# A two-layer streaming encoder on one core: pair matrices and S5 outputs come later, and the last branch's first half is merged between gate products

## The chip, the core and the metric

The kernel runs on one core of a Trainium2 chip, as one program. The engines are TensorE (PE in the profile, its weight loads PEld), VectorE (DVE), ScalarE (ACT), GpSimd (POOL) and SyncE (SP), which issues the loads of the weights. The metric is the device time of one execution in microseconds, and a kernel's time is the median of its runs.

## The reference, cut to what matters

Two layers work on x of 256 rows and 1024 columns. Each layer adds half a feed-forward block, a mixer of four branches, and half a feed-forward block again. The change is in the mixer:

```
def layer_mixer(x):                       # D = 1024, 256 rows, chunk 64
    h = rmsnorm(x, mix_norm[l])
    p = h @ w_in[l]                       # 8*256 columns for the branches + 4*1024 for the gates
    u_a, u_b, r_p, k_p, v_p, z_in, b_g, c_g, gate_pre = jnp.split(p, SPLIT_POINTS, axis=-1)
    y_a = s5_mixer(u_a, ...)              # complex linear recurrence along time, then outputs
    y_b = pool_mixer(u_b, ...)
    y_c = rwkv7_mixer(h, r_p, k_p, v_p, ...)   # delta rule; pairwise products inside a chunk
    y_d = short_conv_mixer(z_in, b_g, c_g, conv_w[l])   # b_g * conv3(c_g * z_in)
    branches = einsum('bsgc,gcd->bsgd', stack([y_a, y_b, y_c, y_d]), w_branch[l])
    gates = sigmoid(gate_pre.reshape(b, s, 4, D))
    merged = sum(branches * gates, axis=2)
    return x + merged @ w_out[l]
```

The branches are numbered 0 (S5), 1 (pool), 2 (RWKV) and 3 (convolution).

## The kernel before

All large products are in fp32, which the kernel makes from two parts: a rounded one (h) and the rest (l). One k-step of 128 rows is three matmuls of 512 columns (`mm3`, L256 to L258): wh with xh, wl with xh, wh with xl. A weight unit is two k-steps of one 512-column half of a weight matrix. SP loads it into one of five raw buffers; ScalarE rounds it to wh (`convert`, L250); `finish` subtracts to get wl, as a rule on VectorE (`tt`, L225). The 256 rows are two tiles t = 0 and 1, and each unit is used by both: four k-steps in all. Four PSUM banks named acc collect these products. Four more, called by `bank()` (pb, gm, sY, tmA and so on), are taken in turn by everything else, so that a new one waits for the reader of the one four before it. Every wl, mg, gate, Gm and Hs instruction that goes through `tt` shows as L225.

The order of the work is made by a planner, `Flow`. It walks a list of steps, one for each unit and row tile, and each k-step is a tick. Beside the steps run threads, generators that give up control and name when they want it back: `wA(n)` n steps later, `wM(n, banks)` n ticks later and only if so many banks are free. What a thread issues stands in every engine's queue at that place. The queues run in order, so an instruction that waits holds all that stand behind it on its engine.

The mixer's steps are the columns of w_in for the branches, two blocks of 256 at a time (the last is bg and cg, the convolution's two gates), then for b = 3, 1, 0, 2 `gate_steps(b)` (the gate's product, two halves hf of 512 columns, with a sigmoid on ScalarE) and `branch_steps(b)` (the projection of the branch by w_branch, two halves). `merge` multiplies a projection with its gate and adds it to mg; for the last branch it then transposes mg and splits it into xh and xl, from which `down` takes the product with w_out.

Threads named in what follows:

- RWKV: W and BK are made on VectorE; the pair matrices gm (L1066) come in two rounds of two banks, sixteen small matmuls each; VectorE masks them into Gm, and POOL copies diagonal blocks into dg (L1077), from which the inverse (inv, L1097) is made much later. tmA and tmB (L1118, L1119) are two rounds of eight transposes; the copies RH (VectorE) and UV (ScalarE) read tmA.
- S5: gA, gB and gt are products on VectorE, followed by two scans (L1373), two products on POOL (gA by TC, gB by TS), Hs on VectorE, and the outputs sY on PE (L1389) in two halves.
- Convolution: zc is cg times z_in on VectorE; cv (L1498) is the sum over three taps, then cv times bg; yl is the rest part of a branch's output.

Of the kernel before, what the change touches and what calls it, by code (L numbers as in the profile page):

```python
# [70 lines left out]
def wM(n=1, banks=0):  # L71

    return ("M", n, banks)
# [98 lines left out]
def trunk_kernel(ctx: ExitStack, tc: tile.TileContext, a, out, dbg=None):  # L172
# [184 lines left out]
    def down(W, nk, lh, ll, scale, gain):  # L357
        P = {}
        ss = {}

        def go(t, hf, u):
            def f():
                if (t, hf) not in P:
                    P[t, hf] = acc()
                    if t not in ss:
                        ss[t] = small.tile([128, 2], F32, name=f"ss{t}", tag=f"ss{t}")
                mmu(P[t, hf], lh(t), ll(t), u, nk)
                if u.k0 + u.nk == nk:
                    args = (t, hf, P[t, hf], scale, ss[t])
                    spawn(next_input(*args, gain) if gain else last_norm(*args))  # L370
            fl.step(f, [u])

        pooled = (1, 3, (0, 0), (2, 0)) if nk == 8 else ()

        def unit(i, k0, hf):
            return Unit(W, k0, 2, hf * 512, 512, gp if i in pooled else ve)

        for k0 in range(0, nk - 4, 2):
            for hf in range(2):
                u = unit((k0, hf), k0, hf)  # L380
                for t in range(2):
                    go(t, hf, u)
        ends = [(hf, unit(i, k0, hf)) for i, (hf, k0) in enumerate((hf, k0) for hf in range(2) for k0 in (nk - 4, nk - 2))]
        if gain:
            for hf, u in ends:
                for t in range(2):
                    go(t, hf, u)
        else:
            for t in range(2):
                for hf, u in ends:  # L390
                    go(t, hf, u)
# [399 lines left out]
    def mixer(l):  # L791
# [110 lines left out]
        def rwkv():  # L902
# [152 lines left out]
            dg = small_tile("dg")  # L1055
            maskb = cc("mask").unsqueeze(1).to_broadcast([128, 4, 128])
            for j in range(2):
                yield wM(4 if j == 0 else 4, 2)
                ps = [bank("gm").rearrange("p (c t) -> p c t", c=4) for _ in range(2)]
                for c in range(4):  # L1060
                    m, o = c // 2, c % 2
                    for e in range(2):
                        es = slice(64 * e, 64 * e + 64)
                        lhs = BK[es, 2 * j + m, 2 * o:2 * o + 2].rearrange("p k t -> p (k t)")
                        rhs = W[es, 2 * j + m, 0:3:2] if o == 0 else W[es, 2 * j + m, 4:6]
                        pe.matmul(ps[e][:, c], lhsT=lhs, rhs=rhs, start=True, stop=True)  # L1066
                yield wA(1)
                for e in range(2):
                    h = 2 * j + e
                    g_ = et([128, 4, 128], f"Gm{h}")  # L1070
                    tt(g_, ps[e], maskb)
                    free()
                    Gm.append(g_)
                    gv = g_.rearrange("p (m o) s -> p o m s", o=2)
                    for q in range(4):
                        qs, cs = slice(32 * q, 32 * q + 32), slice(32 * (q % 2), 32 * (q % 2) + 32)
                        gp.tensor_copy(dg[qs, 2 * h:2 * h + 2], gv[qs, q // 2, :, cs])  # L1077
# [245 lines left out]
        def s5():  # L1323
# [54 lines left out]
            tt(gB, gB, TS, eng=gp)  # L1378
            yield wA(3)
            tt(Hs[:, :, 1:32], gA[:, :, 0:31], gB[:, :, 0:31], ALU.subtract)  # L1380
            yield wM(4, 1)
            pY = bank("sY").rearrange("p (u c) -> p u c", u=4)
            for u in range(4):
                if u == 2:
# [123 lines left out]
        gts = {}  # L1508
        mg = {}

        def gate_steps(b):
            for hf in range(2):
                P = {}

                def ev(t, hf, P):
                    yield wA(1)
                    g_ = st["mp"].tile([128, 512], F32, name="gate", tag="gate", bufs=NG)
                    sc.activation(g_, P[t], AF.Sigmoid, scale=rstd[t])
                    gts[b, t, hf] = g_

                for k0 in range(0, 8, 2):
                    u = Unit(Win, k0, 2, 2048 + b * D + hf * 512, 512)
                    for t in range(2):
                        def f(t=t, u=u, hf=hf, P=P):
                            if t not in P:
                                P[t] = acc()
                            mmu(P[t], lxh(t), lxl(t), u, 8)
                            if u.k0 == 6:
                                spawn(ev(t, hf, P))
                        fl.step(f, [u])  # L1530

        def merge(b, t, hf, p, first, lastb):
# [13 lines left out]
            p = bank()  # L1546
            transposes(p, m_, 4)
            yield wA(1)
            split(xs(xh, t)[:, 4 * hf:4 * hf + 4], xs(xl, t)[:, 4 * hf:4 * hf + 4], p.rearrange("p (a q) -> p a q", q=128))
            free()  # L1550

        def branch_steps(b, first=False, lastb=False):
            for hf in range(2):
                u = Unit(a["w_branch"][l, b], 0, 2, hf * 512, 512)
                for t in range(2):
                    def f(t=t, hf=hf, u=u):
# [16 lines left out]
        branch_steps(1)  # L1573
        gate_steps(0)
        branch_steps(0)
        gate_steps(2)
        branch_steps(2, lastb=True)
        down(a["w_out"][l], 8, lxh, lxl, 1.0, ("ffn2_norm", l))
        fl.step(es_.close, work=False)


# [97 lines left out]
```

## Time and profile before

| | us |
|---|---|
| runs | 1270.63, 1266.59, 1267.92 |
| median | 1267.92 |
| profiled execution | 1268.96 |
| its span, first to last instruction | 1267.2 |

| engine | busy us | share of the span |
|---|---|---|
| PE | 1241.1 | 98% |
| PEld | 1011.4 | 80% |
| DVE | 759.2 | 60% |
| ACT | 618.7 | 49% |
| POOL | 385.1 | 30% |

Times in the rows are counted from the start of the span. Layer 0's mixer does what is changed from about 270 to 310 and from 415 to 440, layer 1's 623 us later. In a timeline row stand the start, the duration, the engine, the line, the operation, the tile written and the tiles read; a bracket at the end gives the idle time before it and what ended it. Matmul rows overlap, since the next one starts while the one before drains: from start to start they take less than the durations say.

### The profile page before, as it was taken

The numbers are of one execution on the slowest core, as the hardware profiler recorded it, in microseconds if no ns is written. First come the engines' busy times: TensorE is split into PE (matmuls) and PEld (weight loads), VectorE is DVE, ScalarE is ACT, GpSimd is POOL, SyncE is SP. The second block draws the span as 40 slices with busy tenths as digits, with TensorE's granted clock in tenths as the row PEclk, the third lists the DMA queues.
The fourth block names the chain that finished last, engine by engine and source line by source line (L and its number), as shares of the span: only waits on it lengthen the run. The fifth ranks groups of instructions, "written<-read, shape, count | busy, mean of one in ns | idle before, by whom it ended". The sixth has DMA issues, their size and how long they took to land.

```text
span 1267.2 us, 19245 instructions
## 1 busy us (share of the span) xinstructions
PE 1241.1 (98%) x7472; PEld 1011.4 (80%) x7472; DVE 759.2 (60%) x935; ACT 618.7 (49%) x787; POOL 385.1 (30%) x512
## 2 busy tenths in 40 slices
PE   7999999999999999999999999999899999999997
PEld 6888878877778788888888888888667787888886
DVE  6955656488556565555465565465974666555543
ACT  5454445655445455443454444466554454544433
POOL 4694383153132310000079453204501233000001
PEclk9999999989999999999999999999999999999999
DMA  8676656544436566666666666566344465666662
GB/s 263 167 223 176 188 161 177 181 128 123 129 117 199 168 182 185 191 175 195 185 186 193 173 186 187 157 189 177 100 126 127 148 184 164 205 190 175 182 198 67
DMA packets 139667, 216.29 MB, mean 171 GB/s; under 512 B 30092, under 2 KB 42232, under 8 KB 139576
## 3 DMA queue, kind: packets, MB, share of 16 engines
q1 hardware_dynamic: 138296, 213.63, 57.1%
q10 hardware_dynamic: 1120, 1.40, 0.3%
q8 instruction: 58, 0.95, 0.3%
q0 software_dynamic: 160, 0.05, 0.1%
q14 instruction: 33, 0.27, 0.1%
HBM read 212.29 MB, written 1.57 MB: 169 GB/s over the span
## 4 chain that ended last, share of the span: by engine, by line
PE 93%; DVE 4%; issue 1%; POOL 1%; DMA 1%; ACT 0%; POOLq 0%; SPq 0%; DVEq 0%; ACTq 0%
PE acc L256 29%; PE acc L258 28%; PE acc L257 28%; PE pb L268 3%; PE inv L1097 1%; DVE wl L225 1%; POOL dg L1077 1%; DVE cv L1498 1%; DVE W L225 0%; PE sY L1389 0%; PE pb L771 0%; DVE rk L1026 0%; DVE mg L225 0%; DMA vr<-in_ffn_norm_dram 0%; PE wu L1202 0%
## 5 line engine op out<-in xcount | busy, mean ns | idle before, releaser
L225 DVE TENSOR_TENSOR wl<-raw,wh 128x1024 fp32r<-128x1024 f32 (+1 forms) x390 | 498.0, 1278 | 302.1 <-ACT wh L250 294.4
L250 ACT ACTIVATE wh<-raw 128x1024 fp32r<-128x1024 f32 (+1 forms) x393 | 414.6, 1056 | 418.7 <-PE acc L258 406.2
L256 PE MATMUL acc<-wh,xh 128*128 128x512 f32 (+1 forms) x1248 | 491.7, 394 | 0.0
L257 PE MATMUL acc<-wl,xh 128*128 128x512 f32 (+1 forms) x1248 | 475.1, 381 | 0.6 <-DVE wl L225 0.6
L258 PE MATMUL acc<-wh,xl 128*128 128x512 f32 (+1 forms) x1248 | 475.1, 381 | 0.0
L256 PEld LDWEIGHTS acc<-wh,xh 128*128 128x128 f32 x1248 | 236.0, 189 | 46.6 <-issue 5.1
L258 PEld LDWEIGHTS acc<-wh,xl 128*128 128x128 f32 x1248 | 236.0, 189 | 45.7
L257 PEld LDWEIGHTS acc<-wl,xh 128*128 128x128 f32 x1248 | 236.5, 190 | 40.9 <-DVE wl L225 1.1
L258 PE MATMUL acc<-wh,hl 128*128 128x512 f32 x352 | 138.7, 394 | 0.0
L256 PE MATMUL acc<-wh,hh 128*128 128x512 f32 x352 | 138.2, 393 | 0.0
L257 PE MATMUL acc<-wl,hh 128*128 128x512 f32 x352 | 138.0, 392 | 0.0
L225 POOL TENSOR_TENSOR wl<-raw,wh 128x1024 fp32r<-128x1024 f32 x11 | 26.4, 2398 | 241.5 <-ACT wh L250 241.5
L256 PEld LDWEIGHTS acc<-wh,hh 128*128 128x128 f32 x352 | 66.1, 188 | 15.2 <-issue 1.3
L257 PEld LDWEIGHTS acc<-wl,hh 128*128 128x128 f32 x352 | 66.2, 188 | 14.6
L258 PEld LDWEIGHTS acc<-wh,hl 128*128 128x128 f32 x352 | 66.2, 188 | 13.3
L429 DVE SCALAR_TENSOR_TENSOR hd<-acc,rs,sg 128x512 f32<-128x512 f32 (+1 forms) x48 | 33.7, 703 | 38.3 <-PE acc L258 36.5
L333 POOL TENSOR_SCALAR pre<-ss 128x1 f32<-128x1 f32 x2 | 0.4, 223 | 173.7 <-ACT junk L281 173.7
L221 ACT ACTIVATE hh<-pb 128x512 fp32r<-128x512 f32 (+1 forms) x48 | 27.0, 563 | 45.4 <-PE pb L268 45.4
L222 DVE TENSOR_TENSOR hl<-pb,hh 128x512 fp32r<-128x512 f32 (+1 forms) x48 | 31.0, 646 | 27.9 <-ACT hh L221 27.5
L225 POOL TENSOR_TENSOR mg<-mg,gate 128x512 f32<-128x512 f32 x16 | 29.9, 1886 | 50.8 <-DVE gate L225 50.8
L422 ACT ACTIVATE sg<-acc,rs 128x512 f32<-128x512 f32 (+1 forms) x48 | 31.1, 653 | 17.8 <-PE acc L258 16.8
L314 ACT ACTIVATE xh<-xg 128x512 fp32r<-128x512 f32 x24 | 15.2, 632 | 30.6 <-DVE xg L225 30.4
(341 smaller groups left out, 1105.5 us busy)
## 6 DMA issues: line engine op xcount, KB each, us to landing
raw<-in_w_in_dram SPq DMA_DIRECT2D x96, 512.0 KB
raw<-in_ffn_w_up_dram SPq DMA_DIRECT2D x88, 512.0 KB
raw<-in_ffn_w_down_dram SPq DMA_DIRECT2D x88, 512.0 KB
raw<-in_ffn_w_gate_dram SPq DMA_DIRECT2D x87, 512.0 KB
raw<-in_w_branch_dram SPq DMA_DIRECT2D x16, 512.0 KB
raw<-in_w_out_dram SPq DMA_DIRECT2D x16, 512.0 KB
x<-in_x_dram SPq DMA_DIRECT2D x2, 512.0 KB
raw<-in_rwkv_g_dram SPq DMA_DIRECT2D x8, 128.0 KB
```

The costliest lines, as they stand in the source:

```text
L221: sc.activation(dh, src, AF.Copy)
L222: eng.tensor_tensor(out=dl, in0=src, in1=dh.bitcast(F32), op=ALU.subtract)
L225: eng.tensor_tensor(out=o, in0=i0, in1=i1, op=op)
L250: sc.activation(self.h, self.r, AF.Copy)
L256: pe.matmul(ps, lhsT=lh, rhs=wh, start=first, stop=False)
L257: pe.matmul(ps, lhsT=lh, rhs=wl, start=False, stop=False)
L258: pe.matmul(ps, lhsT=ll, rhs=wh, start=False, stop=last)
L268: pe.transpose(b[:, j * 128:(j + 1) * 128], src[:, j * 128:(j + 1) * 128], ident)
L314: sc.activation(dh, xg, AF.Copy)
L422: sc.activation(sg[:, :n], pg[:, :n], AF.Silu, scale=rstd[t])
L429: ve.scalar_tensor_tensor(out=hd[:, :n], in0=pu[:, :n], scalar=rstd[t], in1=sg[:, :n], op0=ALU.mult, op1=ALU.mult)
L1077: gp.tensor_copy(dg[qs, 2 * h:2 * h + 2], gv[qs, q // 2, :, cs])
```

## The change

It has four parts.

1. `down`: the list `pooled` is gone. For w_out (`nk == 8`) four units per layer had their wl made on POOL; now all are made on VectorE.
2. Pair matrices: the first round of gm waits for ten ticks and not four, `wM(10, 2)`.
3. S5 outputs: sY waits for nine ticks and not four, `wM(9, 1)`.
4. `gate_steps` and `branch_steps` take the halves to do. Gate 2's first half is done alone; inside gate 2's second half, ahead of its third unit, the first half of branch 2 is projected and merged; its second half follows. The first half's merged result is split into two new tiles `mo` and not into xh and xl, which gate 2's second half still reads; `down` reads `mo` for k below 4.

```diff
-        pooled = (1, 3, (0, 0), (2, 0)) if nk == 8 else ()
 
         def unit(i, k0, hf):
-            return Unit(W, k0, 2, hf * 512, 512, gp if i in pooled else ve)
+            return Unit(W, k0, 2, hf * 512, 512)
...
             for j in range(2):
-                yield wM(4 if j == 0 else 4, 2)
+                yield wM(10 if j == 0 else 4, 2)
                 ps = [bank("gm").rearrange("p (c t) -> p c t", c=4) for _ in range(2)]
...
             tt(Hs[:, :, 1:32], gA[:, :, 0:31], gB[:, :, 0:31], ALU.subtract)
-            yield wM(4, 1)
+            yield wM(9, 1)
             pY = bank("sY").rearrange("p (u c) -> p u c", u=4)
...
-        def gate_steps(b):
-            for hf in range(2):
+        def gate_steps(b, halves=(0, 1), between=None):
+            for hf in halves:
                 P = {}
...
                 for k0 in range(0, 8, 2):
+                    if between and k0 == 4:
+                        between()
                     u = Unit(Win, k0, 2, 2048 + b * D + hf * 512, 512)
...
             p = bank()
             transposes(p, m_, 4)
             yield wA(1)
-            split(xs(xh, t)[:, 4 * hf:4 * hf + 4], xs(xl, t)[:, 4 * hf:4 * hf + 4], p.rearrange("p (a q) -> p a q", q=128))
-            free()
-
-        def branch_steps(b, first=False, lastb=False):
-            for hf in range(2):
+            if not hf and "h" not in mo:
+                mo["h"], mo["l"] = (st["mp"].tile([128, 2, 4, 128], F32R, name=f"mo{i}", tag="f", bufs=NF) for i in range(2))
+            dh, dl = (xs(xh, t)[:, 4:], xs(xl, t)[:, 4:]) if hf else (mo["h"][:, t], mo["l"][:, t])
+            split(dh, dl, p.rearrange("p (a q) -> p a q", q=128))
+            free()
+
+        mo = {}
+
+        def lmo(w, t):
+            xx = xs(xh if w == "h" else xl, t)
+            return lambda k: mo[w][:, t, k] if k < 4 else xx[:, k]
+
+        def branch_steps(b, first=False, lastb=False, halves=(0, 1)):
+            for hf in halves:
...
-        gate_steps(2)
-        branch_steps(2, lastb=True)
-        down(a["w_out"][l], 8, lxh, lxl, 1.0, ("ffn2_norm", l))
+        gate_steps(2, (0,))
+        gate_steps(2, (1,), lambda: branch_steps(2, lastb=True, halves=(0,)))
+        branch_steps(2, lastb=True, halves=(1,))
+        down(a["w_out"][l], 8, lambda t: lmo("h", t), lambda t: lmo("l", t), 1.0, ("ffn2_norm", l))
```

The planner moves more than the lines say. On PE, in layer 0, from the pair matrices to the S5 outputs, before (the k-steps between are left out; a number behind a name tells one tile from another, and the waits are those that stand in the program):

```order
L1066 MATMUL gm_2687<-W_2609,BK_2611 128x128 [waits DVE_49,PE_49]
L1066 MATMUL gm_2688<-W_2609,BK_2611 128x128 [waits PE_49]
...
L823 MATMUL bg_2717<-cst_80,tm_2632 128x128 [waits DVE_49,PE_49,Activation_49]
...
L823 MATMUL cg_2732<-cst_80,tm_2632 128x128 x2
...
L1066 MATMUL gm_2740<-W_2609,BK_2611 128x128 [waits DVE_49]
L1066 MATMUL gm_2741<-W_2609,BK_2611 128x128 [waits DVE_49]
...
L1118 MATMUL tmA_2812<-cst_80,W_2609 128x128 [waits DVE_49]
L1119 MATMUL tmB_2813<-cst_80,KB2_2610 128x128 [waits Activation_49,Pool_49]
...
L1118 MATMUL tmA_2855<-cst_80,W_2609 128x128 [waits DVE_49]
L1119 MATMUL tmB_2856<-cst_80,KB2_2610 128x128 [waits DVE_49]
...
L1389 MATMUL sY_2880<-LK_612,U8_2468 32x128 [waits DVE_49,PE_49,Activation_49]
...
L1389 MATMUL sY_2880<-CA_611,Hs_2775 32x128 [waits DVE_49]
```

and after, where bg and cg come ahead of both rounds of gm, the second bank of the second round (gm_2784) waits for VectorE, and the second round of transposes comes behind sY's first half and waits for VectorE and ScalarE:

```order
L822 MATMUL bg_2687<-cst_80,tm_2632 128x128 [waits PE_49,Activation_49]
...
L822 MATMUL cg_2703<-cst_80,tm_2632 128x128 [waits PE_49]
...
L1065 MATMUL gm_2736<-W_2609,BK_2611 128x128 [waits DVE_49,PE_49]
L1065 MATMUL gm_2737<-W_2609,BK_2611 128x128
...
L1065 MATMUL gm_2783<-W_2609,BK_2611 128x128 [waits Activation_49]
L1065 MATMUL gm_2784<-W_2609,BK_2611 128x128 [waits DVE_49]
...
L1117 MATMUL tmA_2854<-cst_80,W_2609 128x128 [waits DVE_49,Pool_49]
L1118 MATMUL tmB_2855<-cst_80,KB2_2610 128x128 [waits DVE_49,Pool_49]
...
L1388 MATMUL sY_2884<-LK_612,U8_2468 32x128 [waits DVE_49]
...
L1388 MATMUL sY_2884<-CA_611,Hs_2723 32x128 [waits DVE_49]
...
L1117 MATMUL tmA_2904<-cst_80,W_2609 128x128 [waits PE_49]
L1118 MATMUL tmB_2905<-cst_80,KB2_2610 128x128 [waits DVE_49,PE_49,Activation_49]
```

The first round of gm has moved from four k-steps behind the pool branch's products to ten, and sY has come ahead of the second transposes.

On VectorE, at the same place, before:

```order
L225 TENSOR_TENSOR wl_2662<-raw_2482,wh_2661 128x1024 [waits DMAHW6_49,PE_49]
L225 TENSOR_TENSOR Gm0_2697<-gm_2687,cst_80 128x512 [waits PE_49,Pool_49]
L225 TENSOR_TENSOR Gm1_2703<-gm_2688,cst_80 128x512 [waits DMAHW2_49,DMAHW1_49,DMAHW3_49,DMAHW0_49,PE_49]
L225 TENSOR_TENSOR gt_2653<-sX_2629,TS_614 128x512 [waits DVE_49]
L225 TENSOR_TENSOR gA_2651<-gA_2651,gt_2653 128x512 [waits DVE_49]
L1373 SCALAR_TENSOR_TENSOR gB_2652<-R8_615,gB_2652 128x512
L225 TENSOR_TENSOR wl_2712<-raw_2509,wh_2711 128x1024 [waits DMAHW7_49,Activation_49]
L225 TENSOR_TENSOR Gm2_2750<-gm_2740,cst_80 128x512 [waits PE_49,Pool_49]
L225 TENSOR_TENSOR Gm3_2756<-gm_2741,cst_80 128x512 [waits PE_49]
L1373 SCALAR_TENSOR_TENSOR gA_2651<-R8_615,gA_2651 128x512 [waits DVE_49]
L225 TENSOR_TENSOR zc_2788<-cg_2732,zin_2556 128x512
```

and after:

```order
L225 TENSOR_TENSOR wl_2662<-raw_2482,wh_2661 128x1024 [waits DMAHW6_49,PE_49]
L225 TENSOR_TENSOR gt_2653<-sX_2629,TS_614 128x512 [waits DVE_49]
L225 TENSOR_TENSOR gA_2651<-gA_2651,gt_2653 128x512 [waits DVE_49]
L1372 SCALAR_TENSOR_TENSOR gB_2652<-R8_615,gB_2652 128x512
L225 TENSOR_TENSOR wl_2695<-raw_2509,wh_2694 128x1024 [waits DMAHW7_49,Activation_49]
L225 TENSOR_TENSOR zc_2720<-cg_2703,zin_2556 128x512 [waits DMAHW2_49,DMAHW1_49,DMAHW3_49,DMAHW0_49,PE_49]
L1372 SCALAR_TENSOR_TENSOR gA_2651<-R8_615,gA_2651 128x512 [waits DVE_49]
L225 TENSOR_TENSOR Gm0_2746<-gm_2736,cst_80 128x512 [waits PE_49]
L225 TENSOR_TENSOR Gm1_2752<-gm_2737,cst_80 128x512 [waits PE_49]
```

The two rounds of Gm have moved behind the scans and zc, and zc ahead of the second scan.

On VectorE at the last branch of layer 0, before (xl is the split of the transposed mg):

```order
L225 TENSOR_TENSOR gate_4044<-acc_4138,gate_4044 128x512 [waits PE_49,Pool_49]
L225 TENSOR_TENSOR mg00_3072<-mg00_3072,gate_4044 128x512 [waits DVE_49]
L225 TENSOR_TENSOR wl_4136<-raw_4047,wh_4135 128x1024 [waits DMAHW4_49,Activation_49]
L225 TENSOR_TENSOR gate_4055<-acc_4150,gate_4055 128x512 [waits PE_49,Pool_49]
L225 TENSOR_TENSOR mg10_3108<-mg10_3108,gate_4055 128x512 [waits DVE_49]
L222 TENSOR_TENSOR xl_85<-pb_4169,xh_84 128x4x128 [waits Activation_49]
L225 TENSOR_TENSOR gate_4122<-acc_4162,gate_4122 128x512 [waits Pool_49]
L225 TENSOR_TENSOR mg01_3140<-mg01_3140,gate_4122 128x512 [waits DVE_49]
L222 TENSOR_TENSOR xl_85<-pb_4188,xh_84 128x4x128 [waits Activation_49]
L225 TENSOR_TENSOR gate_4133<-acc_4181,gate_4133 128x512 [waits Pool_49]
L225 TENSOR_TENSOR mg11_3176<-mg11_3176,gate_4133 128x512 [waits DVE_49]
L222 TENSOR_TENSOR xl_85<-pb_4208,xh_84 128x4x128 [waits Activation_49]
```

and after:

```order
L225 TENSOR_TENSOR gate_4044<-acc_4098,gate_4044 128x512 [waits PE_49,Pool_49]
L225 TENSOR_TENSOR mg00_3016<-mg00_3016,gate_4044 128x512 [waits DVE_49]
L225 TENSOR_TENSOR wl_4096<-raw_4009,wh_4095 128x1024 [waits DMAHW2_49,Activation_49]
L225 TENSOR_TENSOR gate_4055<-acc_4110,gate_4055 128x512 [waits PE_49,Pool_49]
L225 TENSOR_TENSOR mg10_3046<-mg10_3046,gate_4055 128x512 [waits DVE_49]
L222 TENSOR_TENSOR mo1_4134<-pb_4128,mo0_4133 128x512 [waits Activation_49]
L225 TENSOR_TENSOR wl_4120<-raw_4027,wh_4119 128x1024 [waits DMAHW3_49]
L222 TENSOR_TENSOR mo1_4134<-pb_4146,mo0_4133 128x512 [waits Activation_49]
L225 TENSOR_TENSOR wl_4154<-raw_4047,wh_4153 128x1024 [waits DMAHW4_49,Activation_49]
L225 TENSOR_TENSOR gate_4162<-acc_4178,gate_4162 128x512 [waits PE_49,Activation_49]
L225 TENSOR_TENSOR mg01_3079<-mg01_3079,gate_4162 128x512 [waits DVE_49]
L225 TENSOR_TENSOR wl_4176<-raw_4068,wh_4175 128x1024 [waits DMAHW5_49,Activation_49]
```

There is a weight split, and so a unit of gate 2, between the merging of the first half (mg00, mg10) and that of the second (mg01, mg11), and the first half's rest part goes to mo1.

On the other engines: POOL's two S5 products now stand ahead of the sixteen dg copies, which were ahead of them; and on SP one w_branch load of each layer goes ahead of two loads of w_in.

## Rows read from the trace of the kernel before

**Rows 1.** The page's first part: busy time, share and instructions of each engine.

```profile
PE 1241.1 (98%) x7472; PEld 1011.4 (80%) x7472; DVE 759.2 (60%) x935; ACT 618.7 (49%) x787; POOL 385.1 (30%) x512
```

**Rows 2.** Waits of PE: what waited for what, us in total, times, longest.

```profile
PE gm L1066 <- DVE BK L225: 5.9, 2, 2.9
...
PE sY L1389 <- DVE Hs L225: 3.9, 2, 2.5
PE pb L268 <- DVE mg L225: 2.1, 2, 1.0
```

**Rows 3.** Windows: length, busy time of each engine, granted clock, DMA share, GB/s.

```profile
277.00:284.00 7.00, 6.60 (x29) 5.51 (x30) 6.93 (x12) 0.00 (x0) 1.69 (x4) 0.51 0.42 122
...
298.00:308.00 10.00, 10.00 (x119) 7.75 (x110) 8.49 (x14) 5.93 (x11) 0.00 (x0) 1.00 0.46 123
...
901.00:905.00 4.00, 4.00 (x25) 3.28 (x24) 3.96 (x7) 0.00 (x0) 0.00 (x0) 0.58 0.45 135
...
921.00:926.00 5.00, 5.00 (x63) 3.41 (x54) 3.53 (x6) 2.57 (x7) 0.00 (x0) 0.66 0.37 110
```

**Rows 4.** Timeline of PE, layer 0: start, duration, engine, line, what.

```profile
277.40 2.08 PE L1066 MATMUL gm<-W,BK 64*128 64x128 f32 x16 [2.94 <-DVE BK L225]
...
290.61 0.27 PE L1118 MATMUL tmA<-cst,W 128*128 128x128 f32 x1
...
291.40 0.48 PE L256 MATMUL acc<-wh,xh 128*128 128x512 f32 x1
...
294.23 0.27 PE L1118 MATMUL tmA<-cst,W 128*128 128x128 f32 x1
```

**Rows 5.** Timeline of DVE, layer 0, around the pair matrices and S5.

```profile
272.53 1.79 DVE L225 TENSOR_TENSOR W<-kk,L 128x512 f32<-128x512 f32 x1
...
276.58 0.68 DVE L225 TENSOR_TENSOR BK<-kp,L 128x512 f32<-128x512 f32 x1
...
281.43 1.28 DVE L225 TENSOR_TENSOR Gm<-gm,cst 128x512 f32<-128x512 f32 x2
...
283.96 1.26 DVE L1373 TENSOR_TENSOR_SCAN gB<-R,gB 128x512 f32<-128x512 f32 x1
...
289.48 1.21 DVE L225 TENSOR_TENSOR wl<-raw,wh 128x1024 fp32r<-128x1024 f32 x1
290.61 1.00 DVE L1498 SCALAR_TENSOR_TENSOR cv<-zc,vec,cv 128x255 f32<-128x255 f32 x2
...
293.75 2.91 DVE L1498 SCALAR_TENSOR_TENSOR cv<-zc,vec,cv 128x255 f32<-128x255 f32 x2 [1.32 <-ACT cv L1496]
296.59 1.11 DVE L225 TENSOR_TENSOR Hs<-gA,gB 128x496 f32<-128x496 f32 x1
...
299.89 0.43 DVE L1124 COPY RH<-tmA 64x256 f32<-64x256 f32 x1
```

**Rows 6.** Timeline of POOL, the same stretch.

```profile
287.31 4.39 POOL L1077 COPY dg<-Gm 32x64 f32<-32x64 f32 x8 [0.33 <-DVE Gm L225]
...
293.66 1.28 POOL L225 TENSOR_TENSOR gA<-gA,TC 128x512 f32<-128x512 f32 x1
294.90 1.48 POOL L225 TENSOR_TENSOR gB<-gB,TS 128x512 f32<-128x512 f32 x1
```

**Rows 7.** Timeline of ACT, the second UV copy.

```profile
300.82 0.38 ACT L1126 ACTIVATE UV<-tmA 64x256 f32<-64x256 f32 x1
```

**Rows 8.** Timelines of DVE and POOL, last branch of layer 0.

```profile
420.69 0.68 DVE L225 TENSOR_TENSOR gate<-acc,gate 128x512 f32<-128x512 f32 x1
421.41 2.19 DVE L225 TENSOR_TENSOR mg<-mg,gate 128x512 f32<-128x512 f32 x1
...
420.67 2.39 POOL L225 TENSOR_TENSOR wl<-raw,wh 128x1024 fp32r<-128x1024 f32 x1 [3.06 <-ACT wh L250]
```

**Rows 9.** Windows behind the last branch's first merge; columns as in rows 3.

```profile
424.00:430.00 6.00, 6.00 (x33) 4.71 (x32) 5.88 (x10) 3.69 (x5) 0.00 (x0) 1.00 0.31 91
430.00:440.00 10.00, 10.00 (x46) 8.29 (x45) 2.29 (x2) 4.03 (x4) 4.77 (x2) 1.00 0.75 211
```

## The prediction

> **What bounds the kernel now.** The page's engine line comes first: TensorE (PE) is busy for 1241.1 of 1267.2 us [rows 1], and the change leaves its matmuls as many as they are. So time can only come from where PE waits and from where its clock is low. The waits view, asked for PE alone, is read next [rows 2]: the pair matrices (gm) waited twice for VectorE's BK, 5.9 us together; the S5 outputs (sY) twice for VectorE's Hs, 3.9, the longer one 2.5 and so the other 1.4; and the transposes (pb) of the last branch twice for VectorE's mg, 2.1. All three are what the change touches. Then windows over the stretches where the page's clock line is not at its top [rows 3]: 7 us at a granted clock of 0.51 behind layer 0's gm wait, 4 us at 0.58 behind layer 1's, 5 us at 0.66 behind layer 1's longer sY wait. The lower of the clock's two levels is 1.2 of 2.4 GHz, and the missing share is PE time lost: 0.49 x 7 = 3.4, 0.42 x 4 = 1.7, 0.34 x 5 = 1.7, together 6.8 us. Behind layer 0's sY wait of 1.4 the window is at 1.00, and behind the pb wait too [rows 3, 9]. All that the change can win is thus 5.9 + 3.9 + 2.1 + 6.8 = 18.7 us.
>
> **gm and sY later: what goes.** Both waits of [rows 2] end there, since PE now runs bg, cg and six more k-steps before the first gm, and more before sY. No work is added. In layer 0, PE is free at 277.40 - 2.94 = 274.46 [rows 4]. Until the second gm it has bg and cg, four small matmuls each (eight transposes take 290.61 to 291.40, so 0.4 each); ten k-steps (four take 291.40 to 294.23, 2.83, so 7.1); and the first gm (2.08 at the clock of 0.51, so 1.1 at full clock). That is 9.0, and PE stands at the second gm at 283.4. BK is there from 277.3 [rows 5], so the first gm waits for nothing.
>
> **gm and sY later: what comes instead.** In the new order the second gm takes the bank that cg leaves, and waits for VectorE's zc, which reads cg. VectorE has been without a gap since 272 or earlier. From 281.43, where the first Gm stood, it now does gt, gA and zc (0.68 each, as BK), the first scan (1.26) and a split (1.21): 4.51 by durations [rows 5], so 285.9. Neighbours on VectorE overlap by some 0.07 (two Gm last 1.28, one instruction of their size 0.68), so I take 285.8, the starts being nearer. **PE waits 2.4.** Behind the waiting gm on PE's queue stand six k-steps and the first transposes, none of which anything on VectorE needs soon; so VectorE is not held up by this wait.
>
> VectorE goes on: the second scan to 287.0, two Gm to 288.3. On POOL the two S5 products (1.28 and 1.48, the second ended 2.7 after the first began, [rows 6]) now come ahead of the dg copies, start at the scan's end and end at 289.7. The cv pair behind Gm meets them. Alone a pair takes 1.00, beside the products it took 2.91 and ended 0.3 behind them [rows 5, 6]; so I take 290.0 (289.3 if nothing held it). Then a split 1.2, the second cv pair 1.0, two Gm 1.2, cv x bg 0.65, and Hs 0.65 (the 1.11 of [rows 5] began beside a product): Hs ends at 294.6. PE, from 285.8: gm 1.1, six k-steps 4.2, eight transposes 0.8, three k-steps 2.2, sY's first matmuls 0.2, so 294.3. **Wait at sY: 0.3**, which replaces 1.4 and 2.5.
>
> Next on PE stand the rest of that sY half (0.75) and one k-step (0.8), then the second pair's transposes, at 296.1. One of their banks is that of the first pair's tmA, and waits for two RH copies on VectorE and two UV copies on ScalarE. Before the change that bank was another's. VectorE after Hs: a split 1.2, yl 0.65, a split 1.2, RH twice 0.85, so 298.5 less the overlaps, 298.3; from RH's end (299.89 + 0.43 = 300.32) to UV's end (300.82 + 0.38 = 301.20) it is 0.9 [rows 5, 7]: 299.2. **PE waits about 3.0 there**, a wait that the trace of before does not have (2.6 to 3.2, by overlaps). I find no later one: the dg copies, now behind the products, take 4.4 per eight [rows 6], end near 299, and are read from about 310 on.
>
> So per layer 2.4 + 0.3 + 3.0 = 5.7 of new waits, 11.4 in both (layer 1 has the same order and nearly the same offsets). At the least the cv pair is not held and the two long waits of each layer are 0.7 shorter, 8.6 in all; at the most 3 us more, if VectorE runs as slowly as ahead of this stretch, where W of the same size as BK took 1.79 against 0.68 [rows 5].
>
> **The clock.** The wait of 2.4 may draw a low stretch as those of 2.9 and 2.5 did, worth 1.7 to 3.4. That is PE time ahead of the next two waits, and VectorE does not wait for PE there, so it eats into 0.3 + 3.0 and costs nothing itself. What then remains of the last wait is about 1.5, and the waits of 1.4 and 1.0 drew nothing. If the first draws none, the last, of 3.0, draws one with no cover: 1.7. I charge 1.7 once.
>
> **The last branch.** Its first half is now projected and merged inside gate 2's second half, so each transpose of mg has four k-steps or more between it and its projection; the wait of [rows 2] goes, twice 1.0. The reason for its length lies in POOL: mg took 2.19 while a split of 2.39 ran there (started 0.7 before), against 0.68 for the gate product before it [rows 8]. The eight POOL splits now run on VectorE, 8 x 1.21 = 9.7 us of it, hidden where VectorE is busy 2.29 of 10 us [rows 9]. The merged halves go to new tiles, same instructions. One branch weight load goes ahead of two input loads on SP's queue, per layer; the five raw buffers are loaded well ahead, so nothing. Gain 2.1.
>
> Here a rule can be weighed. While eight dg copies ran on POOL from 287.31 for 4.39, VectorE's split took 1.21 and its cv pair 1.00 [rows 5, 6], no more than elsewhere: no hold. The Trainium skill, SBUF — State Buffer, SBUF: two separate sides, says that VectorE and GpSimd share one port pair as an exclusive lock, so that a VectorE instruction with two SBUF inputs and a GpSimd one that reads SBUF block each other for a whole instruction; the products and the split bear that out, the copies do not. By it the copies, which now run beside Hs and the splits on the path, would hold these up too, as rival C below prices it from rows.
>
> **Sum.** 18.7 - 11.4 - 1.7 = 5.6 us. The profiled execution took 1268.96 (span 1267.2 and 1.76 around it), 1.04 above the median of 1267.92. Taken off the median: 1262.3.
>
> **The rivals.** About 0.3% of the time, 3.8 us, is what a measurement of this kernel can tell from no change, so faster means under 1264.1.
> A: the clock drops uncovered in both layers, at the second transposes. For it: three of three waits of 2.5 and more drew it. Against it: an earlier drop covers it. 18.7 - 11.4 less 2 x 1.7 to 2 x 3.4 leaves 3.9 to 0.5: 1264.0 to 1267.4.
> B: the pair and S5 part gives nothing, since VectorE's total work sets this stretch: it is busy 6.93 of 7 us in the first window of [rows 3], the change takes no work from it there, and PE has six more k-steps to place. Only the last branch remains: 2.1, so 1265.8. It is also the case in which the change does not do what it says. Against it: the second RH ends 2 us earlier in my chain.
> C: the dg copies hold VectorE. Six instructions with two SBUF inputs (two splits, a cv, cv x bg, Hs, yl) stand on the path beside them per layer, each held by one copy (4.39 / 8 = 0.55): 3.3 per layer, 6.6, one more than the sum: 1268.9. Against it: the split and the cv pair of [rows 5] beside the copies of [rows 6].
> D, slower: the splits that leave POOL land on the path. It decides if VectorE has no room around the last branch. It is full there in 5.88 of 6 us ahead of the 2.29 of 10 [rows 9]; if the units of w_out reach it with merges queued ahead of them, each split holds PE for all of its 1.21, and the last branch's gain goes too: 5.6 - 2.1 = 3.5 won, 9.7 lost, 1274.1. Against it: those units follow a stretch of gate products in which VectorE can run ahead.
> E, better: the new waits are half of what I worked out: 1256 to 1259.
>
> **How the numbers follow.** Forecast (1259.5 to 1264.5) 0.45, A 0.24, B 0.12, C 0.05, D 0.06, E 0.08. The range runs from 1259.0 to 1267.4, with the forecast, A and B in it and C, D and E out. Faster: nearly all of the forecast (0.43), E 0.08, and a third of A, where the new waits come out nearer to 8.6 than to 11.4, 0.08: 0.59. Slower: D, 0.06. Same: the rest, 0.35.
>
> **What would show it.** The waits view of after should list gm waiting for zc, about 2.4 twice; the second transposes (tmA or tmB) waiting for RH or UV, 1.5 to 3 twice; sY for Hs under 1; pb for mg not at all; no POOL split of w_out. The clock line should dip once or twice per layer near 286 or 300. A gm that still waits over 1 us for BK, or a second transpose that does not wait, would break the sum; PE waiting for wl behind the last branch would be rival D.

## The result, and the profile after

The changed kernel takes 1262.35 us (median of 4 runs, 1261.19 to 1264.43) against 1267.82 in the same comparison: a ratio of 0.9947, with a 95% interval of 0.9932 to 0.9962. The forecast was 1262.3. Its profiled execution is the one of 1261.19, with a span of 1259.3. In what follows, line numbers of kernels without the list `pooled` are smaller by one.

The page's first part, after [rows 1]:

```profile
PE 1238.6 (98%) x7472; PEld 1010.2 (80%) x7472; DVE 763.9 (61%) x943; ACT 618.3 (49%) x787; POOL 365.6 (29%) x504
```

VectorE has eight instructions more and POOL eight fewer: the weight splits of w_out. The waits of PE after, against [rows 2] (what waited for what; us in total, times, longest):

```profile
PE gm L1065 <- DVE zc L225: 3.6, 2, 1.8
PE tmB L1118 <- ACT UV L1125: 2.7, 2, 1.4
```

All three waits of [rows 2] are gone, and two new ones stand there, both named in the prediction. Layer 0 on PE, then the VectorE and ScalarE instructions that PE waits for (start, duration, engine, line, what; idle before):

```profile
278.95 1.16 PE L1065 MATMUL gm<-W,BK 64*128 64x128 f32 x16
...
282.99 0.48 PE L1065 MATMUL gm<-W,BK 64*128 64x128 f32 x2
285.30 1.52 PE L1065 MATMUL gm<-W,BK 64*128 64x128 f32 x14 [1.82 <-DVE zc L225]
...
295.21 0.42 PE L1388 MATMUL sY<-LK,U 128*32 128x128 f32 x8
...
298.65 0.33 PE L1118 MATMUL tmB<-cst,KB 128*128 128x128 f32 x1 [1.35 <-ACT UV L1125]
```

```profile
284.56 0.69 DVE L225 TENSOR_TENSOR zc<-cg,zin 128x512 f32<-128x512 f32 x1
...
287.46 1.97 DVE L1497 SCALAR_TENSOR_TENSOR cv<-zc,vec,cv 128x255 f32<-128x255 f32 x2
289.36 1.25 DVE L225 TENSOR_TENSOR wl<-raw,wh 128x1024 fp32r<-128x1024 f32 x1
...
293.24 0.71 DVE L225 TENSOR_TENSOR Hs<-gA,gB 128x496 f32<-128x496 f32 x1
...
298.22 0.38 ACT L1125 ACTIVATE UV<-tmA 64x256 f32<-64x256 f32 x1
```

The first gm waits for nothing. The second stops after two matmuls until zc is done at 285.25. sY waits for nothing, since Hs ended at 293.95. The second transposes start when UV ends, at 298.60. The clock in the stretches behind the two gm waits, against [rows 3] (length, busy time of each engine, granted clock, DMA share, GB/s):

```profile
286.00:289.00 3.00, 3.00 (x13) 2.34 (x10) 2.96 (x5) 2.97 (x4) 2.55 (x2) 0.50 0.46 162
907.00:911.00 4.00, 4.00 (x12) 3.16 (x11) 3.96 (x6) 2.22 (x3) 3.92 (x5) 0.57 0.17 67
```

Behind each wait of 1.82 the clock fell to its lower level for a while (a low stretch, below). Each cost PE 1.7: the first window cuts the ends off, and over 285 to 290 the clock is 0.66, so 0.34 x 5 = 1.7, and 0.43 x 4 = 1.7. Behind the shorter waits, of 1.35, there is none. At the last branch, where mg took 2.19 [rows 8], it takes 0.69, and no wait is left:

```profile
412.78 0.68 DVE L225 TENSOR_TENSOR gate<-acc,gate 128x512 f32<-128x512 f32 x1
413.50 0.69 DVE L225 TENSOR_TENSOR mg<-mg,gate 128x512 f32<-128x512 f32 x1
```

**Where the time went, place by place.** The 1664 k-steps (their third matmul, L258, can be counted in the timeline) come in the same order in all kernels here but at the last branch. So the start of the n-th in the profile of before, minus its start in another profile, says how much earlier that kernel is. Differences between five such places give the gain of each stretch, in us:

| kernel | before the first pair stretch | pairs and S5, layer 0 | last branch, layer 0 | pairs and S5, layer 1 | last branch, layer 1 | all |
|---|---|---|---|---|---|---|
| after | 0.46 | 1.98 | 1.32 | 3.14 | 1.33 | 8.23 |
| e0_after | 0.28 | 1.98 | 1.31 | 0.48 | 1.33 | 5.38 |
| e1_pairs | -0.03 | 2.03 | -0.03 | 3.24 | 0.01 | 5.22 |
| e2_last | 0.96 | 0.30 | 1.32 | 1.53 | 1.32 | 5.44 |
| e3_nopool | 0.66 | -2.30 | 0.33 | 1.57 | 0.37 | 0.63 |
| e4_gm_alone | -0.14 | -2.01 | 0.00 | 1.92 | 0.02 | -0.21 |
| e5_gm2_later | -0.11 | 4.26 | 1.32 | 5.48 | 1.32 | 12.28 |
| e6_tm2_later | 1.13 | 3.62 | 1.31 | 5.23 | 1.32 | 12.62 |
| e8_pool_back | -0.23 | 1.97 | -0.84 | 1.72 | -0.83 | 1.81 |
| e9_cover | 0.18 | 4.43 | 1.32 | 5.67 | 1.33 | 12.93 |
| e10_cv_later | 0.09 | 5.84 | 1.31 | 7.03 | 1.33 | 15.61 |

The first column lies ahead of everything that was changed: it is what one execution differs from another at the start. The last column counts to the last k-step. From there to the end of the span it is 7.95 us in before, e1, e4, e8 and e10, and 8.30 in the other seven; why is not known, and spans differ from the table by as much. And a profile is one execution: e2's is the shortest of its twelve runs, those of e0, e4 and e8 are the longest of theirs.

Two things are to be seen ahead of the experiments. The last branch gives the same figure to 0.02 wherever its code is the same. The pair stretch does not: e2 and e3 leave its code as before, and differ from the profile of before by 0.30 and 1.53, and by -2.30 and 1.57. What the clock did goes with the three large ones. In layer 1 of both, the sY waits of 2.4 drew no low stretch, which in the profile of before cost 1.7 [rows 3]. In layer 0 of e3 gm waited 2.94 and the clock stayed at 1.00, so PE came early to sY, waited 3.6 there and not 1.4, and the low stretch came behind that wait. The wait and the windows of e3, layer 0:

```profile
PE sY L1389 <- DVE Hs L225: 6.0, 2, 3.6
```

```profile
277.00:284.00 7.00, 7.00 (x56) 5.60 (x55) 6.93 (x11) 1.66 (x2) 2.31 (x5) 1.00 0.51 150
296.00:302.00 6.00, 5.28 (x60) 3.61 (x61) 4.53 (x7) 2.64 (x6) 0.13 (x1) 0.50 0.28 90
```

### The profile page after: what moved, and what is told of

The parts are those of the page before. It is cut to its first block, busy times and chain, and to the rows that moved or that the text cites. A ratio compares the mean times of both kernels' runs of the same rounds, so it can differ in the third digit from the quotient of the medians.

```text
span 1259.3 us, 19258 instructions
## 1 busy us (share of the span) xinstructions
PE 1238.6 (98%) x7472; PEld 1010.2 (80%) x7472; DVE 763.9 (61%) x943; ACT 618.3 (49%) x787; POOL 365.6 (29%) x504
## 3 DMA queue, kind: packets, MB, share of 16 engines
HBM read 212.29 MB, written 1.57 MB: 170 GB/s over the span
## 4 chain that ended last, share of the span: by engine, by line
PE 93%; DVE 5%; issue 1%; ACT 1%; DMA 0%; POOLq 0%; SPq 0%; POOL 0%; DVEq 0%; ACTq 0%
PE acc L256 29%; PE acc L258 28%; PE acc L257 28%; PE pb L268 3%; DVE wl L225 1%; PE inv L1096 1%; DVE cv L1497 0%; DVE W L225 0%; PE pb L770 0%; DVE rk L1025 0%; PE wu L1201 0%; DVE Gm L225 0%; DMA vr<-in_ffn_norm_dram 0%; PE lr L945 0%; PE pb L766 0%
## 5 line engine op out<-in xcount | busy, mean ns | idle before, releaser
L225 DVE TENSOR_TENSOR wl<-raw,wh 128x1024 fp32r<-128x1024 f32 (+1 forms) x398 | 506.4, 1274 | 298.4 <-ACT wh L250 296.2
L256 PE MATMUL acc<-wh,xh 128*128 128x512 f32 (+1 forms) x1216 | 479.5, 394 | 0.0
L257 PE MATMUL acc<-wl,xh 128*128 128x512 f32 (+1 forms) x1216 | 462.9, 381 | 0.3 <-DVE wl L225 0.3
L258 PE MATMUL acc<-wh,xl 128*128 128x512 f32 (+1 forms) x1216 | 463.1, 381 | 0.0
L256 PEld LDWEIGHTS acc<-wh,xh 128*128 128x128 f32 x1216 | 230.1, 189 | 45.2 <-issue 4.3
L258 PEld LDWEIGHTS acc<-wh,xl 128*128 128x128 f32 x1216 | 229.8, 189 | 44.3
L257 PEld LDWEIGHTS acc<-wl,xh 128*128 128x128 f32 x1216 | 230.4, 189 | 39.4 <-DVE wl L225 0.8
L258 PE MATMUL acc<-wh,hl 128*128 128x512 f32 x352 | 138.9, 395 | 0.0
L225 POOL TENSOR_TENSOR wl<-raw,wh 128x1024 fp32r<-128x1024 f32 x3 | 7.2, 2388 | 253.7 <-ACT wh L250 253.7
L258 PEld LDWEIGHTS acc<-wh,hl 128*128 128x128 f32 x352 | 66.3, 188 | 13.3
```

The lines of the kernel that those rows point to most:

```text
L225: eng.tensor_tensor(out=o, in0=i0, in1=i1, op=op)
L256: pe.matmul(ps, lhsT=lh, rhs=wh, start=first, stop=False)
L257: pe.matmul(ps, lhsT=lh, rhs=wl, start=False, stop=False)
L258: pe.matmul(ps, lhsT=ll, rhs=wh, start=False, stop=last)
```

## The experiments

The theory: each part gives what the table says of it, they add, and PE's position in the pair stretch is set by VectorE's chain (zc, Hs, RH) and by the clock. The rivals: VectorE's total work sets that stretch; the splits taken from POOL cost or give by themselves.

### The changed kernel again

No edit.

> The changed kernel again, unaltered, timed in five rounds. Theory 1 (the gain is read from where the same k-steps stand in the two traces: 2.0 and 3.2 us at the pair matrices and S5 outputs of the two layers, 1.3 at each last branch, 7.8 to 7.9 in all): ratio 0.9938. Theory 2 (the sum of the prediction, 5.6, with a low-clock stretch that nothing covers): ratio 0.9956. In the profile: gm waits for zc 1.8 twice, tmB for UV 1.3 to 1.4 twice, one low-clock stretch of about 3 us behind each gm wait.

Measured: 1261.51 us (1260.25 to 1264.18), ratio 0.9947, between the two theories. The profiled execution is one of the longer ones, with a span of 1262.2, and shows why both are half right. Its waits in layer 1, and its clock there, behind the gm wait and behind the tmB wait:

```profile
PE tmB L1118 <- ACT UV L1125: 2.8, 1, 2.8
PE gm L1065 <- DVE zc L225: 1.8, 1, 1.8
```

```profile
907.00:911.00 4.00, 4.00 (x20) 3.22 (x19) 3.96 (x6) 2.41 (x3) 3.94 (x4) 1.00 0.21 80
919.00:924.00 5.00, 5.00 (x43) 3.78 (x44) 2.25 (x4) 3.14 (x6) 2.65 (x3) 0.50 0.64 199
```

The same gm wait of 1.8 drew no low clock this time. So PE came to the second transposes early, waited 2.8 there, and that wait drew one, which nothing behind it covers: 0.48 instead of 3.14 in the table, 2.7 us. The two cases that the prediction told apart in its part on the clock are both there, in two executions of one kernel.

### Each half alone

```diff
-                yield wM(4 if j == 0 else 4, 2)
+                yield wM(10 if j == 0 else 4, 2)
...
-            yield wM(4, 1)
+            yield wM(9, 1)
```

> The kernel before with the pair matrices and S5 outputs later (wM 10 and 9), the last branch as it was. Theory 1 (parts add, PE's position sets them): 5.2 us faster, ratio 0.9959; gm waits for zc 1.8 twice, tmB for UV 1.35 twice, and pb still waits for mg 1.0 twice. Rival B of the prediction (VectorE's total work sets this stretch): no gain, ratio 1.000.

Measured: ratio 0.9960 (0.9946 to 0.9974), 2.03 and 3.24 in the table. Its waits:

```profile
PE gm L1066 <- DVE zc L225: 3.6, 2, 1.8
PE tmB L1119 <- ACT UV L1126: 2.8, 2, 1.4
PE pb L268 <- DVE mg L225: 2.1, 2, 1.0
```

As theory 1 said; rival B falls. The other half is the change without these two lines:

> The kernel before with the last branch's part alone (first half merged between gate products, weight splits of w_out on VectorE), pair matrices and S5 outputs as they were. Theory 1: 2.6 us faster, ratio 0.9979; gm still waits for BK 2.9 twice and sY for Hs 1.4 and 2.5, pb for mg not at all. Rival D (the splits land on the path): slower than before, PE waiting for wl around the last branch.

Measured: ratio 0.9989 (0.9977 to 1.0001), and 1.32 twice in the table, the 2.6 us that were expected. The expected ratio of 0.9979 lies just inside the interval, and so does 1.0000, no change at all: the times alone do not show this half, the places in the trace do. No wait at pb or for wl is left, the old waits stand:

```profile
PE gm L1065 <- DVE BK L225: 5.9, 2, 3.0
...
PE sY L1388 <- DVE Hs L225: 4.8, 2, 2.4
```

Rival D falls. The two ratios together make 0.9949, the change 0.9947; and place by place e1 has the pair part of the change (2.03 and 3.24 against 1.98 and 3.14), e2 its last branch (1.32 against 1.32 and 1.33). The halves add.

### What makes the last branch's gain

Two edits sit in it: the order, and the splits taken from POOL. First the splits alone:

```diff
-        pooled = (1, 3, (0, 0), (2, 0)) if nk == 8 else ()
+        pooled = ()
```

> The kernel before with one edit: the eight splits of w_out that POOL made are made by VectorE; the order of the last branch is as before. If the POOL split is what lengthened mg (2.19 instead of 0.69): mg takes 0.69, pb waits for mg no more, and nearly all of the last branch's gain comes from this edit alone, 2.1 to 2.6 us, ratio 0.998. If the near order of projection and transpose made the wait: pb still waits for mg about 1 us twice, ratio 1.000.

Measured: ratio 0.9999 (0.9990 to 1.0009), and 0.33 and 0.37 in the table. On VectorE, and in PE's waits:

```profile
423.05 0.69 DVE L225 TENSOR_TENSOR mg<-mg,gate 128x512 f32<-128x512 f32 x1
423.66 0.68 DVE L222 TENSOR_TENSOR xl<-pb,xh 128x512 fp32r<-128x512 f32 x1
```

```profile
PE acc L258 <- DVE xl L222: 0.7, 2, 0.4
PE pb L268 <- DVE mg L225: 0.4, 2, 0.2
```

The POOL split was what lengthened mg, but more than half of the wait came back: with the splits now in its queue, VectorE is late with xl and mg once more, 0.4 and 0.2 in each layer where it was 1.05. Neither expectation held whole: mg takes 0.69, as the first says, and the time stays, as the second says. Then the order alone, the change with the splits back on POOL:

```diff
+        pooled = (1, 3, (0, 0), (2, 0)) if nk == 8 else ()
 
         def unit(i, k0, hf):
-            return Unit(W, k0, 2, hf * 512, 512)
+            return Unit(W, k0, 2, hf * 512, 512, gp if i in pooled else ve)
```

> The changed kernel with the eight splits of w_out back on POOL. If the four k-steps between projection and transpose cover the longer mg: mg takes up to 2.2 where it meets a POOL split, pb waits for nothing, last branches keep their 1.3 us each, ratio 0.9947. If moving the splits is needed: pb or acc waits about 1 us at each last branch, 2 us slower than the changed kernel, ratio 0.9965.

Measured: ratio 0.9976 (0.9966 to 0.9986), and -0.84 and -0.83 in the table: worse at the last branch than the kernel before. Timelines of VectorE and POOL there, and PE's wait:

```profile
414.20 2.19 DVE L225 TENSOR_TENSOR mg<-mg,gate 128x512 f32<-128x512 f32 x1
...
422.14 2.57 DVE L225 TENSOR_TENSOR mg<-mg,gate 128x512 f32<-128x512 f32 x1
```

```profile
413.46 2.38 POOL L225 TENSOR_TENSOR wl<-raw,wh 128x1024 fp32r<-128x1024 f32 x1 [13.44 <-ACT wh L250]
...
421.74 2.41 POOL L225 TENSOR_TENSOR wl<-raw,wh 128x1024 fp32r<-128x1024 f32 x1 [5.90 <-ACT wh L250]
```

```profile
PE pb L268 <- DVE mg L225: 3.5, 4, 1.1
```

The second expectation held in kind: pb waits, by more than it said. The new order puts two merges per layer beside POOL splits, and before there was one; four waits, and not two, are the result. So the four k-steps between projection and transposes do not cover the longer mg. They are not new, either: `merge` asks for `wM(4, 1)` there in both kernels, and where no POOL split is near, the transposes start 1.76 behind the start of mg before the change (the first two rows) and 1.75 behind it after (the others):

```profile
418.95 0.69 DVE L225 TENSOR_TENSOR mg<-mg,gate 128x512 f32<-128x512 f32 x1
420.71 0.60 PE L268 MATMUL pb<-cst,mg 128*128 128x128 f32 x4
411.03 0.69 DVE L225 TENSOR_TENSOR mg<-mg,gate 128x512 f32<-128x512 f32 x1
412.78 0.60 PE L268 MATMUL pb<-cst,mg 128*128 128x128 f32 x4
```

So the two edits need each other: 0.35 and -0.84 alone, 1.32 together.

### What is left of the pair stretch

One of the two lines alone, in the kernel before: the first gm at ten ticks, sY at four.

> The kernel before with the first gm round later (wM 10) and sY as it was (4). Theory (PE waits for VectorE's chain wherever it stands): gm waits for zc about 1.8, sY, which now comes only four k-steps behind the second gm, waits for Hs for most of what the gm wait no longer takes, 4 us or so, and the gain of the pair part is smaller than with both edits (5.2 us): 1 to 4 us, ratio 0.997 to 0.999. If the two edits are independent: the 5.9 us of gm waits less 3.6, and the low clock, 5 us, ratio 0.996.

Measured: ratio 0.9987 (0.9977 to 0.9996), inside what the theory gave. The table has no gain over the two layers (-2.01 and 1.92), but its profile is the longest of ten runs (1269.19, the others 1266.87 to 1267.95): in layer 0 the clock was low behind sY's wait too. Its waits, and that clock:

```profile
PE sY L1389 <- DVE Hs L225: 5.3, 2, 2.7
PE gm L1066 <- DVE zc L225: 3.6, 2, 1.8
```

```profile
295.00:300.00 5.00, 5.00 (x60) 3.32 (x52) 2.54 (x3) 1.17 (x2) 4.71 (x9) 0.50 0.48 127
```

Of the 2.3 us that gm waits less, sY waits 1.4 more (5.3 against 3.9), as the theory said in kind; it had put that at about 4. Next the changed kernel with its second transposes five k-steps later, which is to take away the tmB wait and nothing else:

```diff
-                yield wM(2 if j else 6, 2)
+                yield wM(7 if j else 6, 2)
```

> The changed kernel with the second round of transposes five k-steps behind sY's second half, not ahead of it. Theory: tmB waits for nothing; gm still waits for zc 1.8 twice, and its low-clock stretch, where it comes, now costs its 1.7. Against the changed kernel 1.6 us per layer less where its gm wait drew the low clock and about 4 less where its tmB wait did: 3 to 6 us faster than it, ratio to the kernel before 0.990 to 0.993. Rival: the wait comes back behind it, at akv or for wl, and the time stays, ratio 0.9947.

Measured: 1257.77 us, ratio 0.9910 (0.9893 to 0.9928), as the theory said; the rival falls. Of the waits in this stretch gm's stands, and one of 0.7 for a gate in layer 1:

```profile
PE gm L1065 <- DVE zc L225: 3.7, 2, 1.8
...
PE acc L256 <- ACT gate L1517: 0.7, 1, 0.7
```

And the second gm eight k-steps behind the first:

```diff
-                yield wM(10 if j == 0 else 4, 2)
+                yield wM(10 if j == 0 else 8, 2)
```

> The changed kernel with the second round of gm eight k-steps behind the first and not four; sY then comes ahead of the first transposes. Theory (VectorE's chain sets when Hs and UV are there, and PE waits for it wherever it stands next): gm waits for nothing, sY waits for Hs about 3 us and draws a low clock in some executions; the time stays that of the changed kernel within 1 to 2 us, ratio 0.993 to 0.997. Rival (the gm wait and its low-clock stretch are the cost by themselves): 2 x (2.2 + 1.7) = 7.8 us faster than the changed kernel, ratio 0.9885.

Measured: 1256.73 us, ratio 0.9902 (0.9885 to 0.9919), faster than the theory gave; the rival's 0.9885 is the interval's very end. Its waits:

```profile
PE acc L257 <- DVE wl L225: 3.3, 2, 1.7
...
PE tmB L1118 <- DVE Gm L225: 1.1, 2, 0.6
```

sY does not wait, for two reasons. With the later gm the planner puts two Gm behind Hs on VectorE, not ahead of it, so Hs is earlier; and PE, held 1.7 in each layer by a weight split, comes to it just after Hs has ended, at 293.49:

```profile
292.79 0.70 DVE L225 TENSOR_TENSOR Hs<-gA,gB 128x496 f32<-128x496 f32 x1
293.56 0.41 PE L1388 MATMUL sY<-CA,Hs 128*32 128x128 f32 x8
```

So PE does wait for VectorE wherever it stands next, as the theory said, but for a split and for less: 1.66 and 0.55 per layer, with no low stretch, where the changed kernel has 1.82 and 1.35 and a low stretch. The expectation held VectorE's chain for fixed; it is an order, and it moved too. All three places later (gm 10 and 8, sY 14, transposes 8 and 8):

> The changed kernel with all three places later: second gm eight k-steps behind the first, eight k-steps before the first transposes, sY behind fourteen ticks, second transposes eight ticks after the first. Theory (PE has k-steps enough to run while VectorE finishes its chain): gm, sY and tm wait for nothing, no low-clock stretch, 5.4 us less per layer than the changed kernel's best executions: ratio to the kernel before 0.9865 to 0.988. Rival B of the prediction (VectorE's total work sets this stretch): the waits come back at the k-steps for wl, or at the second transposes, and the ratio stays near 0.9947.

Measured: 1256.12 us, ratio 0.9899 (0.9882 to 0.9916), half of what was hoped for. gm, sY and tm wait for nothing; as rival B said, a wait comes back for wl, but the time does not stay:

```profile
PE acc L257 <- DVE wl L225: 4.2, 4, 1.7
```

```profile
287.75 1.98 DVE L1497 SCALAR_TENSOR_TENSOR cv<-zc,vec,cv 128x255 f32<-128x255 f32 x2
289.65 1.25 DVE L225 TENSOR_TENSOR wl<-raw,wh 128x1024 fp32r<-128x1024 f32 x1
```

The split that PE wants stands behind a cv pair that POOL's products hold to 1.98. The last kernel lets cv come three steps later:

```diff
             tt(zc, got["cg"], zin)
             free()
-            yield wA(1)
+            yield wA(4)
```

> The kernel with all three places later (e9), and the convolution's cv three steps later on VectorE, so that one weight split of PE's next unit stands ahead of both cv pairs. In e9 PE waited there for wl 1.65 and 0.43 in each layer, with the cv pair held to 1.98 beside POOL's S5 products. Theory (VectorE's order inside the stretch, not its total, makes that wait): the long wait goes and the cv pairs take 1.0 each, 1.5 to 2 us less per layer, ratio to the kernel before 0.9865 to 0.988. Rival (VectorE's total work sets it): a wait of the same sum comes at the next wl, ratio as e9, 0.990.

Measured: 1253.00 us (1252.63 to 1253.35), ratio 0.9870 (0.9851 to 0.9890): faster than both kernels, and its runs spread by 0.7 us where those of before spread by 4.7. VectorE:

```profile
287.84 1.36 DVE L225 TENSOR_TENSOR wl<-raw,wh 128x1024 fp32r<-128x1024 f32 x1
...
290.98 1.26 DVE L225 TENSOR_TENSOR wl<-raw,wh 128x1024 fp32r<-128x1024 f32 x1
292.16 0.99 DVE L1497 SCALAR_TENSOR_TENSOR cv<-zc,vec,cv 128x255 f32<-128x255 f32 x2
```

VectorE has the same instructions, in another order, and without the hold on the cv pair. The page of e10:

```profile
PE 1235.9 (99%) x7472; PEld 1005.9 (80%) x7472; DVE 764.7 (61%) x943; ACT 617.4 (49%) x787; POOL 368.9 (29%) x504
```

It is busy 764.7 us there and 763.9 in the changed kernel, which takes some 9 us longer. That settles rival B: the total of VectorE's work does not set this stretch.

## Why the prediction was right, point by point

**What goes.** Right: the three waits of [rows 2] and their low clock are gone.

**The wait at the second gm.** Right in place and cause, 2.4 forecast, 1.82 in the row. PE was to stand there at 283.4 and zc to end at 285.8; with the 0.46 by which all of this profile is earlier, that is 282.9 and 285.3, against 282.99 and 285.25. The row counts idle time only behind the modelled end of the two gm matmuls that still ran; from the first of them to the third it is 285.30 - 282.99 = 2.3.

**The wait at sY.** Forecast 0.3, none came, since the low clock behind the gm wait used up more than that. In e0's layer 1, where there was none, the part of sY that reads Hs starts 0.38 behind the part ahead of it, where 0.24 is usual.

**The wait at the second transposes.** UV was forecast for 299.2, 298.7 with the 0.46, and ended at 298.60. The wait was to be 3.0, or about 1.5 where a low clock ahead of it is covered: 1.35 in this profile, 2.8 in that of e0.

**The clock.** Right as a mechanism; its size is not one number. I charged 1.7 once. Where the gm wait draws the low clock the charge is nought: in layer 1 tmB starts 13.38 behind gm's restart with the low stretch (after) and 13.39 without it (e0). Where the tmB wait draws it, layer 1 gains less than 3.14: 0.48 in e0, and 1.72 in e8, whose code is the same in this stretch and which waited 2.8 there too. That is 2.7 and 1.4, on both sides of 1.7. Layer 1 of e8:

```profile
921.00:925.00 4.00, 3.40 (x22) 2.64 (x26) 2.13 (x3) 2.17 (x5) 3.31 (x4) 0.57 0.51 149
```

In the four profiles with this code (after, e0, e1, e8) six layers of eight have the first case and two the second. Rival A's reason, three of three waits of 2.5 and more, did not last: in e3 a gm wait of 2.94 drew no low clock. What an execution gets is not fixed by the length of the wait, so it is a spread and not a term.

**The last branch.** 2.1 forecast, 2.65 measured (1.32 + 1.33). That the wait goes was right, the first reason given for it was wrong: each transpose of mg had its four k-steps before the change too, and in e8, with the new order and the POOL splits, pb waits as before and more often. The wait goes because mg no longer meets a POOL split. What the order adds is that VectorE has time for the splits that it takes over (e3, without it, waits for xl and mg). The term was taken from the wait column, 1.05 twice. From the start of the last matmul ahead of the transposes to theirs it was 422.31 to 423.75 in the timeline, 1.44 where 0.23 is usual, so 1.21 against the 1.05 that [rows 2] count; the other 0.1 lies at the fourth transposes, which start 0.37 behind the matmul ahead of them (427.23 to 427.60). That POOL's split lengthened mg is shown (0.69 without it in e3, 2.19 and 2.57 with it in e8). That taking it away was enough, as the text can be read, is not so: e3 gained 0.35 per layer.

**The copies and the port.** Beside the dg copies (289.11 to 297.85) the split at 289.36 took 1.25, and two more there took 1.25, against 1.20 to 1.22 ahead of them: held by 0.04, not by a whole copy of 0.55; Hs took 0.71. Rival C falls. The Trainium skill, SBUF — State Buffer, SBUF: two separate sides, says that a VectorE instruction with two SBUF inputs and a GpSimd one that reads SBUF block each other for a whole instruction. The mg rows of e8 agree with that: mg ends at 416.39, 0.55 behind the POOL split that started ahead of it and ended at 415.84. The splits beside the copies do not show it.

**The sum.** The forecast of 5.6 is 0.1 from the medians' 5.5, closer than it earned. Between the two profiled executions the gain was 1268.96 - 1261.19 = 7.8; e0's profile, 1262.2 of span against 1267.2, gives 5.0. The pair part was forecast at 3.5 (18.7 - 2.1 of old cost, less 11.4 and 1.7) and was 5.1 in the one and 2.5 in the other, by the clock that each got; the last branch was forecast 0.5 too small. That the medians fall between is luck of the mixture, as far as two profiles tell. In the first profile two errors stand against each other. The new waits in the column are 6.3 (3.6 and 2.7) and the low stretches 3.4, where 11.4 and 1.7 were forecast; by these columns the pair part would have been 16.6 - 6.3 - 3.4 = 6.9. By place it was 5.1, so about 1.8 lies in neither. A part of it is what the wait column leaves out, as at the second gm; the rest is not traced. For the same reason rival E's condition nearly came (6.3 of 11.4), and its time did not.

## What to carry to other kernels

When a wait is moved, follow the chain of the engine that is waited for to the next place where it is needed, and ask there again; here most places put later brought out another (sY, the second transposes, a weight split), and only the order of VectorE's own queue ended it. Two edits at one place can be worth little or less than nothing apart (0.35 and -0.84 here, 1.32 together), so a part's gain is measured with it alone and with it alone missing. A time from a wait column need not be what the wait costs (1.05 against 1.32 at the last branch): the starts of the same work in two traces give the whole of it, for these two executions.

## What the runs showed of the hardware that I had not expected

The same wait of 1.8 us before layer 1's second gm was followed by a granted clock of 0.57 over 4 us in one execution and of 1.00 in another, with the same instructions around it. In the kernel before, too, the same code stood up to 2.3 us later or 1.6 us earlier per layer in other executions (e3). Over all profiles here, gm's wait of 1.8 was followed by a low clock nine times in twelve, and sY's waits of 2.4 to 2.7 only two times in six. Where PE's waits in this stretch were gone (e10: the longest was 0.3), most of the spread between runs went with them, 4.7 us to 0.7. It was 0.75 in e5 too (four runs each), whose waits of 1.66 and 0.55 drew no low clock in its profile; so the clock behind the waits, more than the waits, seems to go with the spread.
